# Layer 0's projections: from F32R pairs to two scaled F16 parts, with the weights and W_out's rows in a ring of seven places

## Chip, core and metric

The kernel runs on one core of a Trainium2 chip. The metric is the device time of one execution in microseconds (us); lower is better. The engines are named as the profile names them: PE (matrix multiply), PEld (its weight loads), DVE (VectorE), ACT (ScalarE), POOL (GpSimd), and SP, whose queue issues nearly all transfers. Each engine works off its own list of instructions strictly in order.

## What is computed

Two decoder layers on a 1024x1024 input `x` (1024 tokens, width 1024). The change is in layer 0, forgetting attention (FoX) with 16 heads of 64:

```python
h = rmsnorm(x, norm_g[0])
q, k, v, f, z = split(h @ w_in)              # w_in: 1024 x (4*1024 + 16)
c = cumsum(log_sigmoid(f + b_f))             # the forget gate, per head
logits = q @ k.T * 64**-0.5 + c[query] - c[key], causal
x = x + ((softmax(logits) @ v) * silu(z)) @ w_out
```

Layer 1 (native sparse attention) and the final norm follow; the diff changes there only how the square sums of its weights are taken beforehand.

## The kernel before

Every large product is made from two parts of each operand, `hi` and `lo` (`lo` is what `hi` lost in rounding), as three matmuls: hi·hi, hi·lo, lo·hi (`mm3`, L269 to L271 of the profile). In layer 1 both parts are F16, and the weights are first multiplied by a power of two worked out from the root of their square sums, so that they fit F16's range. In layer 0 the parts are F32R, four bytes each, and need no scale.

*Opening.* Eight tiles of 128 tokens are normed (`Norm`, L97 to L109), transposed on PE (L119) and split by `to_hT` into `hT`, the transposed activations (L123 on ACT, L124 on DVE). The order on PE, DVE and ACT is written out by hand here (`manual_schedule`). From tile 5 on, the projection `k0` and the gate (`forget_gate`, matmuls `pf<-hT,wf`) are mixed in.

*Sections.* There are eight head pairs `p`, and four weight sections for each, in the order k, v, q, z: 32 sections of 1024x128. A section is loaded (512 KB), split into `whi` (DVE, L131) and `wlo` (POOL, L134, four pieces), and used in two halves of 512 tokens by `project`: 8 x 3 matmuls of 128x512 for each half, so 48 for a section and 1536 in all. One place `wst` holds the section just loaded; `whi` and `wlo` have two places each.

*Attention.* `fox_main` runs 64 `FoxDuo`s: scores `S` (L767, L768, still F32R), exp (ACT L785), parts `hl` (ACT L786, DVE L787), a transposing transfer (SP L788), and two duos later the product with `v` (`O`, L801 and L802). `merge` puts the projections of later head pairs (`fox_fill`) between the duos by a ratio of costs written in the code; these costs are not changed. The tile framework's scheduler then orders each engine; `late_on` (`keep_in_program_order`) pins an instruction at its place.

*Gate.* After `pf`'s last matmul the gate's values go through a transfer (`fg<-fT`), a chain of small operations on DVE with an Exp and a Ln on ACT (L436 to L454), one tiny matmul `pc<-fg,below` (L457), and DVE L458 and L459. The result `cD` is the bias `B` of the scores.

*Squares.* `early` (class `Squares`) loads W_out and most of layer 1's weights once ahead, 256 KB at a time, for their square sums: ACT L183, which the scheduler places after a small ACT operation (`zg`, L182) on the section's newest result.

*W_out's rows* for layer 0's output product are loaded and converted by `load_wout16` (L703; ACT L712, DVE L714, POOL) into the places of `hT` when the last projections have left them, and `out_start0` begins the product.

Of the kernel before, what the change touches and what calls it, by code (L numbers as in the profile page):

```python
# [41 lines left out]
def tile_fox_nsa(ctx, tc, a, out):  # L42
# [72 lines left out]
    def to_hT(h, t, hT, name, ps=(ps_t, ps_t)):  # L115
        for c in range(2):
            pt = ps[c](f"pth_{name}_{c}")
            for j in range(4):
                T.transpose(pt[:, j * P:(j + 1) * P], h[:, (4 * c + j) * P:(4 * c + j + 1) * P], ident)  # L119
            hi = hT[t // 4][0][:, 4 * c:4 * c + 4, t % 4 * P:(t % 4 + 1) * P]  # L120
            lo = hT[t // 4][1][:, 4 * c:4 * c + 4, t % 4 * P:(t % 4 + 1) * P]
            v = pt.rearrange("p (k t) -> p k t", k=4)
            A.copy(hi, v)  # L123
            V.tensor_tensor(lo, v, f(hi) if hi.dtype == F32R else hi, OP.subtract)  # L124

    def load_w(pool, src, name):
        st = pool.tile([P, KC, P], F32, tag="wst", bufs=1, name=f"wst_{name}")
        dma(st, src)
        hi = pool.tile([P, KC, P], F32R, tag="whi", bufs=2, name=f"whi_{name}")
        lo = pool.tile([P, KC, P], F32R, tag="wlo", bufs=2, name=f"wlo_{name}")  # L130
        V.tensor_copy(hi, st)  # L131
        for k in range(0, KC, 2):
            c = slice(k, k + 2)
            G.tensor_tensor(lo[:, c], st[:, c], f(hi[:, c]), OP.subtract)  # L134
        return hi, lo
# [23 lines left out]
    sums = consts.tile([P, 65], F32, name="sums")  # L159

    class Squares:


        def __init__(self, pool, items, size, bufs):
# [3 lines left out]
        def load(self):  # L168
            if self.items:
                src, col = self.items.pop(0)  # L170
                k, c = src.shape[1:]
                t = self.pool.tile([P, self.size], F32, tag="sq", bufs=self.bufs, name=f"sq_{col}")[:, 0:k * c]
                dma(t.rearrange("p (k c) -> p k c", k=k), src)
                self.at.append((t, col))

        def step(self, x):
            if self.bufs > 1:
                self.load()
            if self.at:
# [3 lines left out]
                A.activation(t, t, AF.Square, bias=z, accum_out=(self.out if col < 8 and self.bufs > 1 else sums)[:, col:col + 1])  # L183
            if self.bufs == 1:
                self.load()
# [18 lines left out]
    def gain_scale(gB):  # L204
# [3 lines left out]
        u = consts.tile([P, 4], F32, name="gain")  # L208
# [4 lines left out]
        V.tensor_scalar(r.bitcast(I32), m.bitcast(I32), 0x7F800000, None, OP.bitwise_xor)  # L213
        V.tensor_scalar(gB, gB, r, 2.0 ** 8, OP.mult, OP.mult)
        V.tensor_scalar(e, m, 2.0 ** -9, None, OP.mult)
# [9 lines left out]

    late_on = tc.keep_in_program_order
# [78 lines left out]
    def channel_scale(sc, n, undo):  # L305
# [8 lines left out]
        V.tensor_scalar(e, e, 2.0 ** -15 * undo, None, OP.mult)  # L314
# [100 lines left out]
    bf = st.tile([H, 1], F32, name="bf")  # L415
    below = st.tile([P, P], F32, name="below")
    wf = st.tile([P, KC, P], F32R, name="wf")
    G.tensor_copy(wf, zero[:, :, None].to_broadcast([P, KC, P]))

    def forget_gate():  # L420
        fT = st.tile([H, S], F32, name="fT")
        f2 = st.tile([H, S], F32, name="f2")
        for half in range(2):
# [6 lines left out]
            V.tensor_copy(f2[:, ts], pt[32:32 + H, :])  # L430
            V.scalar_tensor_tensor(fT[:, ts], pt[0:H, :], bf, f2[:, ts], OP.add, OP.add)
# [33 lines left out]
    def fox_k(p):  # L465
# [3 lines left out]
        for half in range(2):  # L469
# [12 lines left out]
            if p:  # L482
                early.step(pt[:, 0:1])
# [3 lines left out]
    def opening():  # L487
        gB = st.tile([P, D], F32, name="gB")
        xs = []
        for t in range(NT):  # L490
# [4 lines left out]
            if t == 1:  # L495
                wst = wp.tile([P, KC, P], F32, tag="wst", bufs=1, name="wst_k0")
                dma(wst, a["fox_w"][8])
            if t == 3:
                dma(wfst, a["fox_w_f"].rearrange("(k p) c -> p k c", p=P))
                dma(bf, a["fox_b_f"].rearrange("o h -> h o"))  # L500
                dma(below, a["below"])
        dma(tri, a["tri"])
        whi = wp.tile([P, KC, P], F32R, tag="whi", bufs=2, name="whi_k0")
        wlo = wp.tile([P, KC, P], F32R, tag="wlo", bufs=2, name="wlo_k0")
        side = []
        hs = {}
        with tc.manual_schedule(engines={T.engine, V.engine, A.engine}):
            for t in range(NT + 1):
                if t < NT:
                    nm = Norm(st, xs[t], f"n0_{t}", 3)  # L510
                    nm.square(slice(0, D))
                    hs[t] = nm.finish(gB)
                if t:
                    to_hT(hs.pop(t - 1), t - 1, hT, f"n0_{t - 1}", (ps_s, ps_t))
                if t == 1:
                    V.tensor_copy(whi, wst)
                    G.tensor_tensor(wlo, wst, f(whi), OP.subtract)
# [24 lines left out]
    def fox_v(p):  # L542
# [5 lines left out]
        for half in range(2):  # L548
# [27 lines left out]

    def fox_z(p, w, halves=(1, 0)):
# [6 lines left out]
        for half in halves:  # L584
# [1320 lines left out]
```

## Time and profile before

| | |
|---|---|
| median of 3 runs | 1456.75 us (1456.5 to 1458.18) |
| the profiled execution | 1458.12 us; its span, first to last instruction, 1456.2 us |
| PE busy | 1368.0 us, 94% of the span |
| DVE, ACT, POOL busy | 1120.3 (77%), 915.9 (63%), 585.3 us (40%) |
| HBM read | 120.31 MB |

How to read it: a group's row gives its busy time, the mean duration of one, and the idle time of its engine just ahead of it with the instruction that ended it. Matmuls overlap: a matmul's duration is longer than the time until the next one starts, so the pace of PE is read from the starts in the timeline. A row of stages gives the length of the stretch, the busy time of PE, PEld, DVE, ACT and POOL with their instruction counts, the clock that PE was granted, the share of time in which the transfer engines were busy, and GB/s.

### The profile page before, as it was taken

What the parts mean: (1) busy time and instruction counts of PE and PEld (TensorE: products, weight loads), DVE (VectorE), ACT (ScalarE), POOL (GpSimd) and SP (SyncE); (2) the same over time, 40 slices, a digit from 0 to 9 for tenths busy, and PEclk for the clock granted to TensorE, in tenths of its full rate; (3) what the DMA queues carried; (4) which work ended last, traced back from release to release, by engine and by line L of the source; (5) the groups of instructions that cost most, each with busy time, mean ns of one, the idle gap of its engine ahead of it and who ended that gap; (6) DMA issues with size and microseconds to landing.
All of it is one profiled execution on the core that took longest, in us unless ns stands there. A gap on an engine that the chain in (4) does not pass through costs nothing. (4 is left out here: it accounts for less than half of the span.)

```text
span 1456.2 us, 30393 instructions
## 1 busy us (share of the span) xinstructions
PE 1368.0 (94%) x10499; PEld 928.0 (64%) x10499; DVE 1120.3 (77%) x3016; ACT 915.9 (63%) x2328; POOL 585.3 (40%) x781
## 2 busy tenths in 40 slices
PE   5999999999999989999999988889999999998998
PEld 4778888888888745445545544446666766666643
DVE  6587787787878698486757677878999899989834
ACT  5376667776767665155555475667877778778512
POOL 2142433434334251231203456245766766765500
PEclk9999999999999999999999999999999999999999
DMA  5379798898988999354654446454667676776434
GB/s 197 96 164 191 188 185 199 203 186 198 189 197 180 244 230 203 107 176 151 189 174 141 134 121 159 119 148 92 135 151 164 140 171 123 135 169 150 95 109 145
DMA packets 414922, 234.72 MB, mean 161 GB/s; under 512 B 334448, under 2 KB 372656, under 8 KB 414768
## 3 DMA queue, kind: packets, MB, share of 16 engines
q1 hardware_dynamic: 414768, 232.78, 67.1%
q8 instruction: 83, 1.36, 0.4%
q14 instruction: 71, 0.58, 0.1%
HBM read 120.31 MB, written 28.38 MB: 102 GB/s over the span
## 5 line engine op out<-in xcount | busy, mean ns | idle before, releaser
L1662 PE MATMUL S_n<-nk,nq 128*128 128x320 f16 (+5 forms) x768 | 154.6, 314 | 13.5 <-DVE m_n L1670 12.6
L785 ACT ACTIVATE P<-P,m 128x512 f32<-128x512 f32 (+1 forms) x192 | 116.3, 607 | 53.9 <-DVE m L776 52.6
L1677 POOL TENSOR_TENSOR hl_n<-P_n,hl_n 128x640 f16<-128x640 f32 (+4 forms) x128 | 144.8, 1132 | 10.0
L756 POOL TENSOR_TENSOR Bd<-B,tri 128x128 f32<-128x128 f32 x128 | 62.4, 502 | 205.8 <-DVE m L776 189.3
L787 DVE SCALAR_TENSOR_TENSOR hl<-P,hl 128x512 f16<-128x512 f32 (+1 forms) x192 | 116.0, 620 | 28.7 <-ACT hl L786 27.2
L1676 POOL CAST hl_n<-P_n 128x640 f16<-128x640 f32 (+4 forms) x128 | 76.4, 597 | 122.1 <-ACT P_n L1673 97.3
L1673 ACT ACTIVATE P_n<-P_n,m_n 128x640 f32<-128x640 f32 (+7 forms) x128 | 98.7, 771 | 30.2 <-DVE m_n L1670 29.6
L1673 ACT ACTIVATE P_n<-P_n,m_n,units 128x640 f32<-128x640 f32 (+4 forms) x128 | 100.1, 782 | 22.5 <-DVE m_n L1672 20.6
L1662 PEld LDWEIGHTS <-nq 128*128 128x128 f16 x768 | 71.4, 98 | 60.4 <-issue 25.5
L286 ACT ACTIVATE pth_n<-ptp_n 128x512 f16<-128x512 f32 (+1 forms) x160 | 85.1, 545 | 38.9 <-PE ptp_n L1695 38.3
L287 DVE SCALAR_TENSOR_TENSOR ptl_n<-ptp_n,pth_n 128x512 f16<-128x512 f32 (+1 forms) x160 | 99.6, 632 | 7.9 <-ACT pth_n L286 5.9
L1695 PE MATMUL ptp_n<-ident,P_n 128*128 128x128 f32 x576 | 93.2, 279 | 7.5 <-ACT P_n L1673 2.2
L786 ACT ACTIVATE hl<-P 128x512 f16<-128x512 f32 (+1 forms) x192 | 92.4, 512 | 1.9 <-DMA pT<-hl 0.5
L1670 DVE CUSTOM_DVE_ANT_0 P_n<-S_n,wmask 128x640 f32<-128x640 f32 (+4 forms) x128 | 83.1, 650 | 7.2 <-PE S_n L1662 6.3
L1695 PEld LDWEIGHTS ptp_n<-ident,P_n 128*128 128x128 f32 x576 | 64.9, 141 | 33.4 <-DVE ptl_n L287 7.3
L183 ACT ACTIVATE sq<-sq,zg 128x512 f32<-128x512 f32 (+2 forms) x73 | 59.5, 815 | 22.8 <-DMA sq<-in_nsa_w_dram 17.8
L1703 PE MATMUL O_n<-nv,pth_n 128*128 128x64 f16 x576 | 71.7, 193 | 1.0 <-ACT pth_n L286 0.6
L97 ACT ACTIVATE h_n<-xr 128x512 f32<-128x512 f32 x32 | 20.0, 625 | 83.6 <-DVE xr L1795 41.4
L1704 PE MATMUL O_n<-nv,pth_n 128*128 128x64 f16 x576 | 71.8, 193 | 0.0
L1670 DVE CUSTOM_DVE_ANT_0 P_n<-S_n,bias,units 128x640 f32<-128x640 f32 (+1 forms) x64 | 68.8, 1074 | 2.9 <-PE S_n L1662 2.3
L1705 PE MATMUL O_n<-nv,ptl_n 128*128 128x64 f16 x576 | 68.7, 193 | 0.9 <-DVE ptl_n L287 0.9
L767 PE MATMUL S<-KH,Q 128*128 128x512 f32 (+1 forms) x192 | 65.0, 354 | 2.6 <-DVE m L776 2.3
(514 smaller groups left out, 4731.6 us busy)
## 6 DMA issues: line engine op xcount, KB each, us to landing
sq<-in_nsa_w_dram SPq DMA_DIRECT2D x40, 256.0 KB
B<-cD SPq DMA_DIRECT2D x16, 512.0 KB
nq<-qD SPq DMA_DIRECT2D x64, 128.0 KB
x<-in_x_dram SPq DMA_DIRECT2D x8, 512.0 KB
wst_k<-in_fox_w_dram SPq DMA_DIRECT2D x8, 512.0 KB
wst_v<-in_fox_w_dram SPq DMA_DIRECT2D x8, 512.0 KB
sq<-in_fox_w_out_dram SPq DMA_DIRECT2D x16, 256.0 KB
wst_q<-in_fox_w_dram SPq DMA_DIRECT2D x8, 512.0 KB
```

The lines of the kernel that those rows point to most:

```text
L286: A.activation(hi[:, 0:n], pt[:, 0:n], AF.Copy, scale=scale)
L287: V.scalar_tensor_tensor(lo[:, 0:n], pt[:, 0:n], scale, h, OP.mult, OP.subtract)
L785: A.activation(L[:, 0:n], L[:, 0:n], AF.Exp, bias=init, scale=-1.0, accum_out=self.lr[:, col + c:col + c + 1])
L786: A.activation(hi[:, cs], L[:, 0:n], AF.Copy, scale=UP)
L787: V.scalar_tensor_tensor(lo[:, cs], L[:, 0:n], UP, hi[:, cs], OP.mult, OP.subtract)
L1662: T.matmul(ps[:, b, 0:w], self.q[x][:, qi * P:(qi + 1) * P], k[:, k0 + b * w:k0 + b * w + w], start=(x == 0), stop=(x == 1))
L1670: V.tensor_tensor_reduce(dst, src, mk, 1.0 if y else unit, 3e38, OP.add, OP.min, m)
L1673: A.activation(L, L, AF.Exp, bias=m, scale=minus if y else -1.0, accum_out=self.l[:, y, qi:qi + 1])
L1676: G.tensor_copy(hl[:, 0:n], L)
L1677: G.tensor_tensor(hl[:, n:2 * n], L, hl[:, 0:n], OP.subtract)
L1695: T.transpose(pt[:, (x + i) * P:(x + i + 1) * P], L[:, kb * P - k0:(kb + 1) * P - k0], ident)
L1704: T.matmul(o, hi, v[:, 64:128], start=False, stop=False)
```

## The change

- `hT` becomes F16, and `to_hT` multiplies by a scale from the largest gain: `gain_scale(gB, 0)`, one reduction and five small DVE operations, now in the opening.
- Each weight section is scaled as it is split, by `split_w16`: DVE makes `hi` with a multiply; POOL multiplies the section in place and then subtracts (four pieces each). `k0`'s section is split on DVE alone.
- The scale of a head pair's four sections comes from their square sums: `ring_square` (ACT, 128x1024, one for each section), `ring_total` (ACT cast, a PE matmul with `ones`), `ring_scale` (five small DVE operations). The inverse is applied where q, k, v and z are read out of PSUM, in operations that were there before; k's and q's together in q's.
- Sections and, after them, the eight 512 KB pieces of W_out's rows go through `ring`, seven places of 4 KB per partition; `issue()` loads the next item. `conv_wout` converts W_out's rows straight from the ring.
- `early` loads 512 KB at a time, pinned squares without the `zg` operation, half as many.

```diff
-    hT = [[hp.tile([P, KC, 512], F32R, ...) for i in range(2)] for x in range(2)]
+    hT = [hp.tile([P, 2, KC, 512], F16, tag=f"h{x}", name=f"hT0_{x}") for x in range(2)]
...
+    def issue():
+        if len(ring) < len(items):
+            src, name = items[len(ring)]
+            ring.append(hp.tile([P, KC, P], F32, tag=f"r{len(ring) % 7}", name=f"wst_{name}"))
+            dma(ring[-1], src)
...
+    def ring_square(n):
+        j = sa.tile([P, D], BF16, tag="sq", bufs=1, name=f"wj_{n}")
+        late_on(A.activation(j, ring[n]..., AF.Square, accum_out=wu[n // 4][:, n % 4:n % 4 + 1]))
+    def ring_total(p, x, y):
+        A.copy(tb[:, x:y], wu[p][:, x:y])
+        late_on(T.matmul(pt[:, x:y], ones, tb[:, x:y], start=True, stop=True))
+    def split_sec(n):
+        return split_w16(ring[n], wu[n // 4][:, 5 + n % 4:6 + n % 4], parts, n > 0)
...
+    def tick(second):
+        n = sect[0]
+        if second:
+            if n % 4 == 2 and n < 28:
+                ring_scale(n // 4 + 1, 0, 4, totals.pop())
+            early.load()
+            sect[0] += 1
+        else:
+            if n + 6 < 32:
+                ring_square(n + 6)
+            early.square()
+            if n % 4 == 2 and n < 28:
+                totals.append(ring_total(n // 4 + 1, 0, 4))
...
             if p == 0:
-                for _ in range(11):
+                issue()
+                early.load()
+                for n in (1, 2, 3):
+                    ring_square(n)
+                    for _ in range(3):
+                        yield next(gate0)
+                pt = ring_total(0, 1, 4)
+                for _ in range(2):
                     yield next(gate0)
+                ring_scale(0, 1, 4, pt)
...
-                rows0 = load_wout16(hp, "fox_w_out", 1, 200, 2)
-                yield next(rows0)
+                rows0 = conv_wout(1, 200, 2)
```

The place that moves most is the start of head pair 0's v. On PE, before: the last of the gate's matmuls, then v's; `pc` stands behind all 48 of v's matmuls.

```order
L427 MATMUL pf_395<-hT_1_0_103,wf 128x512
L428 MATMUL pf_395<-hT_1_1_104,wf 128x512
L269 MATMUL v_0_457<-hT_0_0_101,whi_v_439 128x512
L270 MATMUL v_0_457<-hT_0_1_102,whi_v_439 128x512
L271 MATMUL v_0_457<-hT_0_0_101,wlo_v_440 128x512
...
L457 MATMUL pc<-fg_418,below 128x1
L269 MATMUL q_1_545<-hT_1_0_103,whi_q_448 128x512
```

PE at the same place now (F16 weights are loaded by an instruction of their own; `wsum` is `ring_total`'s matmul):

```order
L493 MATMUL pf_442<-hT_1_102,wf 128x512
L427 LDWEIGHTS ones
L427 MATMUL wsum_1_465<-wtb_1_463,ones 128x3
L522 MATMUL pc<-fg_473,below 128x1
L267 LDWEIGHTS whi_v_503
L267 MATMUL v_0_529<-hT_0_101,whi_v_503 128x512
L268 LDWEIGHTS whi_v_503
L268 MATMUL v_0_529<-hT_0_101,whi_v_503 128x512
L269 LDWEIGHTS wlo_v_504
L269 MATMUL v_0_529<-hT_0_101,wlo_v_504 128x512
```

`wsum` and `pc` moved ahead of v's 48 matmuls.

DVE there before: the gate's chain ends (L454), and the split of z follows; v's and q's had been made long before.

```order
L453 SCALAR_TENSOR_TENSOR fg_418<-fg_417,fg_416 128x4
L454 TENSOR_TENSOR fg_415<-fg_415,fg_418 128x96
L131 CAST whi_z_538<-wst_z_536 128x1024
L458 COPY fg_416<-pc 128x1
L459 TENSOR_SCALAR fg_415<-fg_415,fg_416 128x128
```

DVE now (`wu` holds the sums and scales of the sections):

```order
L518 SCALAR_TENSOR_TENSOR fg_473<-fg_472,fg_471 128x4
L519 TENSOR_TENSOR fg_470<-fg_470,fg_473 128x96
L436 TENSOR_SCALAR wu_103<-wsum_1_465 128x3
L523 COPY fg_471<-pc 128x1
L437 TENSOR_SCALAR wu_103<-wu_103 128x3
L439 TENSOR_SCALAR wu_103<-wu_103,gain_162 128x3
L438 TENSOR_SCALAR wu_103<-wu_103 128x3
L524 TENSOR_SCALAR fg_470<-fg_470,fg_471 128x128
L441 SCALAR_TENSOR_TENSOR wu_103<-wu_103 128x2
L140 TENSOR_SCALAR whi_v_503<-wst_v_140,wu_103 128x1024
```

The scales of v, q and z, and with them v's `hi`, stand behind the gate's whole chain.

In the opening, DVE between tile 3's norm and tile 4's before (`st_n` and `h_n` are a tile's norm; `k0`'s one cast stands further ahead, its `lo` was POOL's):

```order
L109 SCALAR_TENSOR_TENSOR h_n_3_187<-x_120,st_n_3_186,gB 128x1024
L124 TENSOR_TENSOR hT_0_1_102<-pth_n_2_0_192,hT_0_0_101 128x4x128
L124 TENSOR_TENSOR hT_0_1_102<-pth_n_2_1_199,hT_0_0_101 128x4x128
L105 RECIPROCAL st_n_4_206<-st_n_4_206 128x1
L109 SCALAR_TENSOR_TENSOR h_n_4_207<-x_125,st_n_4_206,gB 128x1024
```

The same stretch now (`fu` holds the scales of `k0` and of the gate's weights):

```order
L128 SCALAR_TENSOR_TENSOR hT_0_101<-pth_n_2_1_228,gain_162,hT_0_101 128x4x128
L593 TENSOR_SCALAR fu<-wsum_235 128x2
L595 TENSOR_SCALAR fu<-fu 128x2
L596 TENSOR_SCALAR fu<-fu 128x2
L597 TENSOR_SCALAR wu_103<-fu,gain_162 128x1
L598 TENSOR_SCALAR wu_103<-fu,gain_162 128x1
L140 TENSOR_SCALAR whi_k_242<-wst_k_122,fu 128x1024
L149 SCALAR_TENSOR_TENSOR wlo_k_243<-wst_k_122,fu,whi_k_242 128x512 x2
L105 RECIPROCAL st_n_4_247<-st_n_4_247 128x1
L109 SCALAR_TENSOR_TENSOR h_n_4_248<-x_131,st_n_4_247,gB 128x1024
```

Eight operations on `k0`'s weights and scales now stand ahead of tile 4's norm. In the rest of layer 0 the order of projections, scores and products on PE stays as it was but for a handful of matmuls that change places with a neighbour.

More of the change, by code (lines that the diff above doesn't have):

```diff
@@ L122, in to_hT @@
             v = pt.rearrange("p (k t) -> p k t", k=4)
[L123 to L135, printed above, removed]
+            if scale is None:
+                A.copy(hi, v)
+                V.tensor_tensor(lo, v, hi, OP.subtract)
+            else:
+                A.activation(hi, v, AF.Copy, scale=scale)
+                V.scalar_tensor_tensor(lo, v, scale, hi, OP.mult, OP.subtract)
     def load_w16(staged, src, name, scale, gp=False):
@@ L202, in roots, with gain_scale @@
         return r
-    def gain_scale(gB):
-        u = consts.tile([P, 4], F32, name="gain")
+    def gain_scale(gB, layer):
+        u = (consts if layer else hp).tile([P, 4], F32, name=f"gain{layer}")
         m, r, e, b = (u[:, i:i + 1] for i in range(4))
@@ L482, in fox_k @@
             if p:
-                early.step(pt[:, 0:1])
+                tick(half)
         ready["k", p] = KH, KL
@@ L646, in fox_fill @@
                 assert not early.at
-                first.append(roots(sums[:, 0:41], ((0, 4), (4, 8), (8, 24), (24, 40), (40, 41)), "early"))
-                ready["o7"] = hp.tile([P, NT, 2, P], F16, tag="h11", name="o7_0")
-                yield from out_start0(load_wout16(hp, "fox_w_out", 0, 200, 0))
+                first.append(roots(sums[:, 0:21], ((0, 2), (2, 4), (4, 12), (12, 20), (20, 21)), "early"))
+                issue()
+                ready["o7"] = hp.tile([P, NT, 2, P], F16, tag="r0", name="o7_0")
+                yield from out_start0(conv_wout(0, 200, 0))
     xs0 = {}
     def out_start0(rows1):
-        yield next(rows1)
         parts = [(t, 0, 4) for t in (4, 5, 6, 7)] + [(t, 4, 7) for t in (4, 5, 6, 7)] + [(t, 0, 7) for t in (0, 1, 2)]
@@ L695, in out_start0, with conv_rows, conv_wout @@
                 yield 1000
+    def conv_rows(src, w, half, pace, vrows):
+        for k in range(4):
+            r = 4 * (1 - half) + k
+            sc = ready["wscale"][:, r:r + 1]
+            for c in range(2):
+                yield pace
+                cs = slice(c * 512, c * 512 + 512)
+                A.activation(w[:, 0, k, cs], src[k][:, cs], AF.Copy, scale=sc)
+                if c or k < vrows:
+                    V.scalar_tensor_tensor(w[:, 1, k, cs], src[k][:, cs], sc, w[:, 0, k, cs], OP.mult, OP.subtract)
+                else:
+                    G.tensor_scalar(src[k][:, cs], src[k][:, cs], sc, 1.0, OP.mult, OP.mult)
+                    G.tensor_tensor(w[:, 1, k, cs], src[k][:, cs], w[:, 0, k, cs], OP.subtract)
+        ready.setdefault("wout", []).append((w[:, 0], w[:, 1]))
+    def conv_wout(half, pace, vrows):
+        src = [ring[36 - 4 * half + k].rearrange("p k c -> p (k c)") for k in range(4)]
+        w = hp.tile([P, 2, 4, D], F16, tag=f"h{half}", name=f"wo0_{half}")
+        yield from conv_rows(src, w, half, pace, vrows)
     def load_wout16(pool, src, half, pace, vrows):
```

167 lines of the change are left out of this document (102 added, 65 removed).

## The prediction

> **What bounds the kernel now.** I read the stages first, then who waited for whom on PE in layer 0, then the timeline for PE's pace, and last the gate's chain, because the order shows that PE will wait for it. The stages (columns: window, length, busy PE, PEld, DVE, ACT, POOL, then the clock, the transfer engines' share, GB/s):
>
> ```profile
> span 1456.2 us, 30393 instructions
> 110.00:500.00 390.00, 389.67 (x2427) 316.38 (x2426) 299.18 (x947) 270.07 (x720) 142.83 (x218) 1.00 0.87 193
> 500.00:590.00 90.00, 77.88 (x517) 46.23 (x516) 73.43 (x231) 51.22 (x130) 25.36 (x34) 0.94 1.01 232
> 1000.00:1300.00 300.00, 287.80 (x3690) 204.11 (x3690) 273.60 (x748) 232.61 (x547) 197.68 (x237) 1.00 0.68 143
> ```
>
> From 110 to 500 us PE is busy without a gap, DVE 77%, ACT 69%, POOL 37%. In those 390 us PE waited once (columns: engine and line, for whom, total, times, longest):
>
> ```profile
> PE z L271 <- POOL wlo_z L134: 0.2, 1, 0.2
> ```
>
> So there PE's own pace sets the time, and what makes its matmuls start closer together is gained in full until another engine is late. Its pace is read from starts (start, duration), F32R first, F16 below:
>
> ```profile
> 45.11 0.40 PE L427 MATMUL pf<-hT,wf 128*128 128x512 f32 x1
> 48.61 0.40 PE L428 MATMUL pf<-hT,wf 128*128 128x512 f32 x1
> 48.84 0.39 PE L269 MATMUL v<-hT,whi_v 128*128 128x512 f32 x1
> 714.14 0.38 PE L270 MATMUL pn_qr<-hT,whi_nqr 128*128 128x512 f16 x1
> 720.83 0.38 PE L271 MATMUL pn_qr<-hT,wlo_nqr 128*128 128x512 f16 x1
> ```
>
> Between the first and second row lie 15 intervals: 3.50/15 = 0.2333 us. Between the two F16 rows lie 31: 6.69/31 = 0.2158. An F16 matmul of this shape thus costs PE 0.0175 us less.
>
> The Trainium skill, "TensorE: Matmul & The Clock Gate", section "Back-to-back issue gap", gives N/2.4 + 2.5 ns for a warm array and no term for the data type; that is 216 ns for 512 columns. F16 agrees with it; F32R, by 0.2333 us, does not. By the rule the change would gain nothing in pace; by the rows it does, and the rows decide.
>
> **Part 1: up to q0's start, +14.2.** The time lost is in the start of head pair 0. The gate's chain before:
>
> ```profile
> 49.76 0.74 DVE L431 SCALAR_TENSOR_TENSOR fT<-pf,bf,f 16x512 f32<-16x512 f32 x1
> 53.24 0.29 DVE L436 SCALAR_TENSOR_TENSOR fg<-fg 128x128 f32<-128x128 f32 x1 [2.74 <-DMA fg<-fT]
> 55.97 1.28 ACT L443 ACT_TABLE_LOAD   x1
> 57.61 0.29 DVE L444 TENSOR_TENSOR fg<-fg,fg 128x128 f32<-128x128 f32 x1 [1.88 <-ACT fg L443]
> 59.40 0.26 DVE L454 TENSOR_TENSOR fg<-fg,fg 128x96 f32<-128x96 f32 x1
> 60.04 0.28 PE L457 MATMUL pc<-fg,below 128*128 128x1 f32 x2
> 60.18 0.48 PE L269 MATMUL q<-hT,whi_q 128*128 128x512 f32 x1
> 60.86 0.85 DVE L459 TENSOR_SCALAR fg<-fg,fg 128x128 f32<-128x128 f32 x1
> 605.34 0.15 DVE L211 TENSOR_SCALAR gain<-gain 128x1 f32<-128x1 f32 x1
> ```
>
> Before, v's 48 matmuls (48.84 to 60.04) covered this chain, and nobody on PE saw it. Now `pc` and v's split stand behind it, so the cover is gone: PE finishes `pf`, and then waits for all of it.
>
> (a) The opening. DVE gets the gain's reduction and five small operations, five more for `k0`'s scale, and two subtractions that POOL did. What it loses is a stall: POOL's long subtraction ran at 13.28, and DVE's norm of a tile beside it took 3.40 us where the next one took 1.28.
>
> ```profile
> 13.28 2.34 POOL L517 TENSOR_TENSOR wlo_k<-wst_k,whi_k 128x1024 fp32r<-128x1024 f32 x1 [10.70 <-DVE st_n L105]
> 13.31 3.40 DVE L109 SCALAR_TENSOR_TENSOR h_n<-x,st_n,gB 128x1024 f32<-128x1024 f32 x1
> 18.01 1.28 DVE L109 SCALAR_TENSOR_TENSOR h_n<-x,st_n,gB 128x1024 f32<-128x1024 f32 x1
> 604.10 1.21 DVE L210 TENSOR_REDUCE gain<-gB 128x1 f32<-128x1024 f32 x1
> 9.92 0.17 DVE L105 RECIPROCAL st_n<-st_n 128x1 f32<-128x1 f32 x1 [1.44 <-ACT st_n L104]
> L183 ACT ACTIVATE sq<-sq,zg 128x1024 f32<-128x1024 f32 x16 | 18.4, 1148 | 0.4
> L183 ACT ACTIVATION_READ_ACCUMULATOR sq<-sq,zg 128x1 f32 x73 | 13.6, 187 | 0.0
> L787 DVE SCALAR_TENSOR_TENSOR hl<-P,hl 128x512 f16<-128x512 f32 (+1 forms) x192 | 116.0, 620 | 28.7 <-ACT hl L786 27.2
> ```
>
> Added on DVE: 1.21 + 10 x 0.15 + 2 x 0.62 = 3.95; gone: 3.40 - 1.28 = 2.12; so +1.8. Of it the idle 1.44 ahead of tile 1's reciprocal may hide most (+0.4). On ACT one 1024-wide square with its read (1.15 + 0.19) and a few small operations (the gate's square, two casts, about 0.8 at a quarter of a us each) stand ahead of tile 3's norm: up to +2.1 more, so +0.4 to +3.9. I take +3.0, near the upper end, since DVE and ACT both have little air there. Some 70 F16 matmuls until `pf`'s end give back 70 x 0.0175 = 1.2. `pf` ends at 48.84 + 1.8 = 50.6.
>
> (b) The wait. From `pf`'s end to the end of L454: 59.66 - 48.84 = 10.8. The Ln's table load stood behind v's readout on ACT, which now comes later, so DVE's idle 1.88 goes: 8.9. Then the scales: six small operations, with issue about 0.19 each (1.1), L524 (the L459 of before: between 0.29, the chain's other 128x128 operations, and its own 0.85 beside POOL's work; 0.4, as POOL is idle now), and v's `hi`, 0.75:
>
> ```profile
> L147 DVE TENSOR_SCALAR whi_nqr<-wst_nqr,roots_early x6: 752/755/1192, 706.5 to 793.1; 128x1024 f16<-128x1024 f32 x6
> L151 POOL TENSOR_SCALAR wst_nv<-wst_nv,roots_late x16: 476/482/906, 809.4 to 852.2; 128x256 f32<-128x256 f32 x16
> L152 POOL TENSOR_TENSOR wlo_nv<-wst_nv,whi_nv x16: 666/674/1116, 810.3 to 853.3; 128x256 f16<-128x256 f32 x16
> L134 POOL TENSOR_TENSOR wlo_z<-wst_z,whi_z x32: 731/741/1200, 60.9 to 481.1; 128x256 fp32r<-128x256 f32 x32
> ```
>
> Together 11.2; at least 10.2, with the scales wholly beside other work, at most 13.5, if the 1.88 stays and L524 takes 0.85. v's first matmul: 50.6 + 11.2 = 61.8.
>
> (c) v itself. Its third matmul needs POOL's first `lo` piece, 0.48 + 0.48 + 0.67 = 1.6 after `hi`, and after eleven idle us PE starts at half clock, as `k0` did:
>
> ```profile
> 23.92 0.78 PE L269 MATMUL k<-hT,whi_k 128*128 128x512 f32 x1
> 28.27 0.40 PE L270 MATMUL k<-hT,whi_k 128*128 128x512 f32 x1
> ```
>
> Ten intervals there took 4.35 instead of 2.33: +2.0. The two overlap; I take +2.2 for both (2.0 to 3.6). All of v then: 48 x 0.2158 + 2.2 = 12.6, q0's start at 74.4 against 60.18: **+14.2**, with the bounds above +10.4 to +18.
>
> **Part 2: PE's pace from there on, -29.7.** Left are 1536 - 48 (k0) - 48 (v0) = 1440 projection matmuls: 1440 x 0.0175 = **-25.2**. Besides, a weight load of F32R is long, and the first projection after a product pays for it:
>
> ```profile
> 301.92 0.19 PE L802 MATMUL O<-v,pT 128*128 128x64 f16 x1
> 301.95 0.49 PE L269 MATMUL q<-hT,whi_q 128*128 128x512 f32 x1
> 302.27 0.40 PE L270 MATMUL q<-hT,whi_q 128*128 128x512 f32 x1
> L269 PEld LDWEIGHTS q<-hT,whi_q 128*128 128x128 f32 x128 | 24.4, 190 | 5.4
> L269 PEld LDWEIGHTS <-whi_nqr 128*128 128x128 f16 x96 | 9.6, 100 | 10.6 <-issue 1.1
> ```
>
> 0.32 instead of 0.233 us; the F16 load is shorter by as much, 0.09. The order has 52 such passages: **-4.5** (between nothing and that; the load's difference accounts for all of it). The scores stay F32R.
>
> **Part 3: the other engines in that stretch, +4.** ACT: in these 390 us 50 squares of 512 with their reads and `zg` cost 50 x (0.724 + 0.187 + 0.2) = 56; now some 25 early and 28 ring squares of 1024, 53 x 1.34 = 71, and a few casts: 270 + 17 = 287 of 360.
>
> ```profile
> L183 ACT ACTIVATE sq<-sq,zg 128x512 f32<-128x512 f32 x50 | 36.2, 724 | 18.6 <-DMA sq<-in_nsa_w_dram 15.9 <-DMA sq<-in_fox_w_out_dram 1.4
> ACT sq L183 <- DMA sq<-in_nsa_w_dram: 17.8, 9, 6.3
> ```
>
> DVE: 299 + 7 x 5 x 0.15 = 304 of 360, 85%. POOL: for each section 4 x (0.48 + 0.67 - 0.74) = 1.6 more, 26 sections: +43, 186 of 360; it came late for PE once in 390 us, by 0.2 (above), so this alone delays nobody. `ring_total`'s cast stands on ACT a section ahead of its matmul, and that matmul costs PE a narrow slot seven times. The transfers stay the same in bytes; half as many square loads go through SP. In layer 1 DVE at 91% (273.60 of 300) goes with 4% of idle PE, while at 77% in layer 0 there is none. Between, at 85% of 360, I take 1%: **+4** (0 to 14).
>
> **Part 4: the end of layer 0, -1.5.** From 500 to 590 PE idles 90 - 77.88 = 12 us. W_out's 4 MB now come earlier, and two squares fewer stand in ACT's way; the conversions are as many. -5 to +1.
>
> **Sum:** 14.2 - 25.2 - 4.5 + 4 - 1.5 = -13.0 on the profiled execution's 1458.12: 1445.1. That execution lies 1.4 above the median of the runs, 1456.75; on that scale 1443.7, said as **1444**.
>
> **Rivals.** *R1, the full gain:* no engine is late (+0), the opening hides its work and the start costs +11: 1456.75 + 11 - 29.7 - 3 = 1435. For it: PE's single wait in 390 us. Against: the order, which leaves nothing beside the chain.
>
> *R2, DVE becomes the second bound:* POOL's extra 43 us block DVE as at 13.31 us. If every us did, DVE would have 304 + 43 = 347 of 360, above layer 1's 91%, where 4% of PE was idle: +14 instead of +4, so 1454. For it: the 3.40. Against: that was one 1024-wide operation beside DVE's own; POOL's pieces are 0.5 to 0.7 long. The skill's "SBUF — State Buffer", section "Who interferes with whom", says that such operations hold a shared port to their end; the 3.40 agrees, and no run here counts how often.
>
> *R3, slower: the squares' loads come late.* 512 KB are now asked for half a section (390/26/2 = 7.5 us) before a pinned square, where 256 KB were; ACT waits in order, and the exps behind it. Before, nine squares waited 17.8 us, the longest 6.3. ACT's 287 leave 73 of 360; slower than before it would get when the 25 early squares wait over (73 + 13)/25 = 3.5 us each. At 4.5: ACT's stretch is 287 + 112 = 399, so nothing of part 2 is left: 1456.75 + 14.2 + 9 - 1.5 = 1478; at 3.7 about 1460.
>
> *R4, no change in pace in layer 0:* F32R's 0.2333 comes from something that F16 shares there: 1456.75 + 14.2 - 4.5 + 4 - 1.5 = 1469. This is what the clock-gate page's rule would give. Against: the same interval at 45 us and 300 us, in streams of different content.
>
> **How the numbers follow.** The forecast, PE's pace less the gate's wait, 1437 to 1451: 60%. R1 14%, R2 14%, R3 7%, R4 2%, others 3%. Changes of up to 0.2% (2.9 us) are about what a measurement cannot tell from none: faster means below 1453.8. Forecast and R1 are faster; R2 straddles the line (6 faster, 5 same, 3 slower); so 81% faster, 6% same, 13% slower. The range, 1431 to 1456, takes in R1, the forecast's bounds and most of R2 and leaves out R3 and R4.
>
> **What would show it.** PE idle for about 11 us near 51 to 62 us, released by DVE's `hi` of v or by `pc`; intervals of 0.216 in q, k, v, z; PE still without gaps of note from 120 to 470; ACT's waits for the squares' transfers below 1 us each. Wrong would be: PE waiting for DVE or ACT all through the stretch, intervals of 0.233, or v starting near 50.

## The result, and the profile after

The changed kernel takes 1469.95 us, median of five runs (1466.27 to 1473.78), where the kernel before took 1456.75 (1455.81 to 1459.36) beside it: ratio 1.0085, interval 1.0062 to 1.0108. It is slower by 0.85%; the forecast was 0.9% faster. The profiled execution took 1467.63 us, 9.5 more than the one before.

The page after (span and busy times), and the two stages of layer 0 (columns as before):

```profile
span 1465.8 us, 30457 instructions
PE 1342.5 (92%) x10508; PEld 786.3 (54%) x10508; DVE 1130.9 (77%) x3069; ACT 933.7 (64%) x2291; POOL 648.7 (44%) x904
110.00:500.00 390.00, 370.53 (x2444) 205.87 (x2443) 312.26 (x996) 278.51 (x678) 204.75 (x331) 1.00 0.90 195
500.00:590.00 90.00, 82.94 (x574) 47.33 (x573) 80.26 (x254) 55.30 (x138) 26.47 (x36) 0.98 0.88 191
```

PE is busy 25.5 us less in sum and the kernel is longer all the same. From 110 to 500 us PE did 370.53 of 390 where it had done 389.67: it got its faster matmuls, and stood still for 19.5 us where it had stood still for 0.3.

One ruler serves for all that follows. It is the view of one tile, `wlo_q` on PE; each row has min, median and longest duration (ns), then the start of the first and of the last such matmul. The first lies at q0's start, the last near the end of the projections. Before, then after:

```profile
L271 PE MATMUL q<-hT,wlo_q x128: 389/392/632, 60.7 to 514.2; 128*128 128x512 f32 x128
L269 PE MATMUL q<-hT,wlo_q x128: 377/379/379, 73.9 to 523.9; 128*128 128x512 f16 x128
```

The first starts 13.2 later. The stretch from first to last is 450.0 where it was 453.5: 3.5 shorter, where PE's pace alone (part 2) was worth 29.7. The last starts 9.7 later, and so does the end, by 9.5. So the loss is the start's, which was forecast, plus some 26 us in the stretch, of which 4 were forecast. The row of the whole stretch, before and after (columns as before):

```profile
60.70:514.20 453.50, 449.74 (x2773) 364.51 (x2772) 344.88 (x1103) 312.80 (x833) 164.49 (x254) 1.00 0.87 194
73.90:523.90 450.00, 425.18 (x2780) 235.09 (x2779) 353.20 (x1133) 318.61 (x776) 226.65 (x366) 1.00 0.87 190
```

PE's busy time fell by 24.6 us, and its idle time rose from 3.8 to 24.8: 21 of the 26 are waits.

The start, from PE's timeline after (start, duration, in brackets the idle time and who ended it):

```profile
48.62 0.38 PE L493 MATMUL pf<-hT,wf 128*128 128x512 f16 x1
51.51 0.16 PE L427 MATMUL wsum<-wtb,ones 128*128 128x3 bf16 x1 [2.52 <-ACT wtb L425]
57.56 0.56 PE L522 MATMUL pc<-fg,below 128*128 128x1 f32 x2 [5.88 <-issue]
59.57 0.61 PE L267 MATMUL v<-hT,whi_v 128*128 128x512 f16 x1 [1.45 <-DVE whi_v L140]
61.66 0.61 PE L269 MATMUL v<-hT,wlo_v 128*128 128x512 f16 x1 [1.06 <-POOL wlo_v L145]
73.51 0.38 PE L267 MATMUL q<-hT,whi_q 128*128 128x512 f16 x1
```

PE waits for the sums, for the gate's chain (put down to "issue": what it needs came just before), for `hi`, and for POOL's first `lo`, and begins v at half clock (0.61 us for a matmul of 0.38).

What PE waited for from 110 to 500 us, after; before, there was one wait of 0.2 us in all:

```profile
PE O L903 <- DMA pT<-hl: 9.7, 7, 3.1
PE O L903 <- DVE m L878: 3.6, 2, 2.6
PE S L869 <- DVE m L878: 2.5, 6, 0.9
```

The largest part is the product `O` waiting for its transposing transfer `pT`. These transfers stand in SP's queue, and so do the loads of sections. SP's own waits in the same window, first before, then after (rows for POOL's `lo` of k, v and z only):

```profile
SPq L128 <- POOL wlo_k L134: 14.1, 6, 3.2
SPq L128 <- POOL wlo_v L134: 11.0, 6, 2.9
SPq L128 <- POOL wlo_z L134: 8.8, 5, 2.3
```

```profile
SPq L413 <- POOL wlo_k L145: 21.0, 6, 4.5
SPq L413 <- POOL wlo_z L145: 19.0, 7, 5.8
SPq L413 <- POOL wlo_v L145: 10.7, 5, 3.1
```

33.9 us have become 50.7. A load takes the place of the section that POOL is just splitting, and may be issued only when POOL's last `lo` piece is done. POOL's work on a section is longer now (POOL was busy for 204.75 us of the window where it had been for 142.83), so the load, and each transposing transfer behind it in the queue, goes out later. One such case in the timeline, after:

```profile
277.26 1.34 DVE L889 SCALAR_TENSOR_TENSOR hl<-P,hl 128x512 f16<-128x512 f32 x2
278.84 1.30 POOL L145 TENSOR_TENSOR wlo_k<-wst_k,whi_k 128x256 f16<-128x256 f32 x2
280.16 0.33 SPq L413 DMA_DIRECT2D wst_z<-in_fox_w_dram  x1
280.58 3.44 SPq L890 DMA_TRANSPOSE pT<-hl  x1
286.11 0.23 PE L903 MATMUL O<-v,pT 128*128 128x128 f16 x1 [1.20 <-DMA pT<-hl]
```

`hl` is ready at 278.60; POOL's pieces end at 280.14; SP issues the load, and the transposing transfer only at 280.58, two us after its data. At 286.11 the product waits 1.20 us. A duo has two such issues; over duos 10 to 50 of the 64 they came 0.55 us after their data on average before, and 1.47 after.

### The profile page after: what moved, and what is told of

Read it like the earlier page. It is cut to its first block, busy times and chain, and to the rows that moved or that the text cites. A ratio compares the mean times of both kernels' runs of the same rounds, so it can differ in the third digit from the quotient of the medians.

```text
span 1465.8 us, 30457 instructions
## 1 busy us (share of the span) xinstructions
PE 1342.5 (92%) x10508; PEld 786.3 (54%) x10508; DVE 1130.9 (77%) x3069; ACT 933.7 (64%) x2291; POOL 648.7 (44%) x904
## 5 line engine op out<-in xcount | busy, mean ns | idle before, releaser
L858 POOL TENSOR_TENSOR Bd<-B,tri 128x128 f32<-128x128 f32 x128 | 66.1, 531 | 161.2 <-DVE m L878 116.2
L869 PE MATMUL S<-KH,Q 128*128 128x512 f32 (+1 forms) x192 | 76.7, 414 | 5.7 <-DVE m L878 2.5
L903 PE MATMUL O<-v,pT 128*128 128x128 f16 x576 | 58.5, 221 | 19.6 <-DMA pT<-hl 16.0
## 6 DMA issues: line engine op xcount, KB each, us to landing
sq<-in_nsa_w_dram SPq DMA_DIRECT2D x28, 512.0 KB
B<-cD SPq DMA_DIRECT2D x16, 512.0 KB
x<-in_x_dram SPq DMA_DIRECT2D x8, 512.0 KB
wst_k<-in_fox_w_dram SPq DMA_DIRECT2D x8, 512.0 KB
wst_v<-in_fox_w_dram SPq DMA_DIRECT2D x8, 512.0 KB
wst_q<-in_fox_w_dram SPq DMA_DIRECT2D x8, 512.0 KB
wst_z<-in_fox_w_dram SPq DMA_DIRECT2D x8, 512.0 KB
```

## The experiments

The table has every run: its time, its ratio to the kernel before beside it, and the ruler. (Ratios compare best between rows; the kernel before itself ran at 1456.75 to 1458.67 us beside them. The ruler is read from one profiled execution of each kernel, so differences of two or three us between its rows say little.)

| kernel | us | ratio (interval) | q0 | last | stretch |
|---|---|---|---|---|---|
| before | 1456.75 | 1 | 60.7 | 514.2 | 453.5 |
| after | 1469.95 | 1.0085 (1.0062 to 1.0108) | 73.9 | 523.9 | 450.0 |
| f16only | 1440.80 | 0.9868 (0.9846 to 0.9889) | 58.1 | 499.4 | 441.3 |
| noscale | 1456.52 | 0.9986 (0.9967 to 1.0006) | 75.2 | 514.2 | 439.0 |
| early0 | 1460.98 | 1.0017 (0.9998 to 1.0036) | 65.2 | 518.1 | 452.9 |
| spread | 1463.22 | 1.0033 (1.0017 to 1.0049) | 75.0 | 522.0 | 447.0 |
| even | 1477.33 | 1.0129 (1.0102 to 1.0156) | 73.9 | 536.4 | 462.5 |
| evenf16 | 1455.83 | 0.9977 (0.9963 to 0.9991) | 57.7 | 518.1 | 460.4 |
| poolmul | 1461.81 | 1.0018 (1.0003 to 1.0034) | 57.9 | 515.7 | 457.8 |
| poolwst2 | 1457.48 | 0.9995 (0.9982 to 1.0008) | 57.8 | 514.5 | 456.7 |
| f16wst2 | 1437.99 | 0.9869 (0.9847 to 0.9892) | 58.4 | 494.0 | 435.6 |
| later | 1468.31 | 1.0071 (1.0045 to 1.0097) | 75.5 | 528.5 | 453.0 |
| comb | 1453.04 | 0.9963 (0.9950 to 0.9976) | 63.6 | 508.8 | 445.2 |
| nomul | 1456.25 | 0.9977 (0.9959 to 0.9995) | 73.7 | 512.5 | 438.8 |
| gpq | 1468.38 | 1.0060 (1.0036 to 1.0084) | 75.7 | 523.5 | 447.8 |
| poolgpq | 1458.56 | 1.0007 (0.9985 to 1.0028) | 58.6 | 512.0 | 453.4 |
| f16gpq | 1447.43 | 0.9914 (0.9886 to 0.9941) | 58.7 | 503.4 | 444.7 |
| combnomul | 1435.28 | 0.9846 (0.9811 to 0.9880) | 61.4 | 493.0 | 431.6 |
| f16sq64 | 1434.97 | 0.9830 (0.9800 to 0.9860) | 58.0 | 493.3 | 435.3 |

PE's pace alone would make the stretch 453.5 - 29.7 = 423.8.

**F16 alone (f16only).** The kernel before, with F16 for `hT`, `whi`, `wlo` and `wf`, no scales and no ring; each engine's instructions keep their order.

```diff
-hT = [[hp.tile([P, KC, 512], F32R, ...
+hT = [[hp.tile([P, 2, KC, 512], F16, ...)[:, 0] ...
-hi = pool.tile([P, KC, P], F32R, tag="whi", ...)
+hi = pool.tile([P, 2, KC, P], F16, tag="whi", ...)[:, 0]
```

> The kernel before with one thing changed: hT, whi, wlo and the gate's weights are F16 instead of F32R, without any scales, squares, ring or moved work (its small parts lose accuracy, its instructions are those of before). Theory A, the vector engines' pace: in a run of duos DVE and ACT need about 6.9 us for a duo, as much as PE needed with F32R, so a faster PE only waits: PE idles 10 to 20 us between 110 and 500 us, where it idled 0.3, and the time is 1437 to 1447. Theory B, the added work is to blame: without it PE follows at its F16 pace, idles under 5 us there, and the time is 1425 to 1433.

16 us faster, and 2.6 of it before q0 (on the ruler). Its stretch is 12.2 shorter, not 29.7: more than half of the pace was lost with none of the change's added work there. Its window from 110 to 500 us, its last 19.4 us of the stretch, what PE waits for in the window, and what ACT waits for most:

```profile
110.00:500.00 390.00, 374.43 (x2463) 208.53 (x2462) 300.24 (x971) 275.82 (x740) 136.06 (x220) 0.99 0.92 203
480.00:499.40 19.40, 13.09 (x81) 6.39 (x80) 12.15 (x47) 11.51 (x32) 1.77 (x4) 0.82 1.06 290
PE total_o L243 <- ACT sb_o L241: 5.9, 1, 5.9
PE S L767 <- DVE m L776: 2.4, 6, 1.0
PE O L801 <- DMA pT<-hl: 2.2, 3, 1.5
ACT sq L183 <- DMA sq<-in_nsa_w_dram: 24.1, 9, 6.4
```

15.6 us idle: PE now arrives before DVE, ACT and what they feed. The largest wait is a single one: at 493.47 PE stands 5.9 us for a total that layer 0's output product needs, and around it the granted clock fell too (0.82 in the last 19.4 us). The rest is short waits. The averages (DVE 77%, ACT 71%) hide a lag that may be behind them, since the work of those engines comes in runs. The eight duos of a run follow each other every 6.9 us before, and at F16's pace every 6.4 where PE doesn't wait; then, about 16 us after the last duo's start, the next run begins. Within a run DVE and ACT fall behind: the time from a duo's last score to its last `hl`, averaged over the five runs of duos 10 to 49, grows from 5.1 us at a run's first duo to 7.4 at most before (6.6 over all); in f16only from 5.7 to 8.4 (7.6 over all), and after from 6.0 to 9.0 (8.1 over all, the longest 10.5). The window of one run before shows no more than this:

```profile
226.00:270.00 44.00, 44.00 (x285) 35.83 (x284) 34.14 (x113) 33.34 (x90) 11.47 (x20) 1.00 0.90 200
```

DVE at 78%, ACT at 76%: neither is full even there. They take turns in a duo (maximum, exp, `hl`), so each waits for the other, and a chain can fall behind before an engine is full. A rival stands beside this: ACT, in order, waits in f16only for the transfers of the early squares, with the exps behind them, for 25.5 us of the 390 (the 24.1 above and 1.4 for W_out's; 17.3 before). No run here takes that away from f16only.

**Three things taken out of the changed kernel.** *noscale:* head pairs 1 to 7 use head pair 0's scales, so the ring's squares, sums and scales go.

```diff
-ring_scale(n // 4 + 1, 0, 4, totals.pop())
-ring_square(n + 6)
-totals.append(ring_total(n // 4 + 1, 0, 4))
-return split_w16(ring[n], wu[n // 4][...
+return split_w16(ring[n], wu[0][...
```

> The changed kernel without the squares, sums and scales of the sections from head pair 1 on (they use head pair 0's scales): 28 squares of 1024 on ACT, 28 reads, 7 casts, 7 matmuls and 35 small DVE operations are gone. Theory A: the loop of DVE and ACT over a duo is little shorter, PE's idle between 110 and 500 us falls from 19.5 to 12 to 18, the time to 1462 to 1468. Theory B: it falls under 6, the time to 1453 to 1457.

13 us gained; on the ruler 11 of it in the stretch (439.0 from 450.0).

*early0:* head pair 0's squares stand ahead of `k0`'s end, and its scales ahead of most of the gate's chain.

```diff
+for n in (1, 2, 3): ring_square(n)
 yield from k0
-for n in (1, 2, 3): ring_square(n) and three steps of the gate each
+three steps of the gate
 pt = ring_total(0, 1, 4)
-two steps of the gate
 ring_scale(0, 1, 4, pt)
+eight steps of the gate
```

> The changed kernel with head pair 0's three squares ahead of k0's end and its sum and scales ahead of the gate's chain, so that v's split no longer stands behind it. If the wait at the start costs what the trace shows (v's first matmul 59.6 instead of 48.8, and some 2 us at half clock), q0 starts at 60 to 63 instead of 73.5 and the time falls by 9 to 13, to 1457 to 1461. The rival, that the time is given back at the first scores, because the gate's result or the vector engines are late then: 1463 to 1469.

9 us gained, most of the price of the order at the start: q0 comes 8.7 us earlier on the ruler, at 65.2, still 4.5 later than before. In its timeline v begins right behind the gate's matmuls again (the last of them starts at 49.76); what is left are a wait of 1.14 us for POOL's first `lo` at 51.71, and `pc`'s:

```profile
47.36 0.17 PE L427 MATMUL wsum<-wtb,ones 128*128 128x3 bf16 x1
49.98 0.38 PE L267 MATMUL v<-hT,whi_v 128*128 128x512 f16 x1
64.08 0.40 PE L522 MATMUL pc<-fg,below 128*128 128x1 f32 x2 [2.27 <-DVE fg L518]
```

*spread:* the early square moves from the half in which the ring's square stands to the other half.

```diff
 early.load()  # second half's tick
+  ahead of it: early.square()
 ring_square(n + 6)  # first half's tick
-early.square()
```

> The changed kernel with its two 1024-wide squares of a section in different halves of it, instead of one behind the other. If a block of 2.5 us on ACT ahead of the exps makes PE wait, PE's idle between 110 and 500 us falls from 19.5 to under 12 and the time by 6 to 10, to 1460 to 1464. If ACT's and DVE's sum over a run of duos counts, it is within 3 us of the changed kernel, 1467 to 1472.

6.7 us gained. In the changed kernel the two squares stood together on ACT, ahead of the exps:

```profile
96.40 1.04 ACT L421 ACTIVATE wj<-wst_v 128x1024 bf16<-128x1024 f32 x1
97.44 1.04 ACT L174 ACTIVATE sq<-sq 128x1024 f32<-128x1024 f32 x1
98.48 0.50 ACT L887 ACTIVATE P<-P,m 128x256 f32<-128x256 f32 x1
100.39 0.29 PE L903 MATMUL O<-v,pT 128*128 128x128 f16 x1 [3.69 <-DMA pT<-hl]
```

The exp of the next duo starts two us late, and a product finds its transfer missing in the same stretch.

**More even spacing (even, evenf16).** Other numbers in the ratio of costs, on the changed kernel and on f16only: a wider spacing of the duos and a shorter stretch of lone projections at a pair's end.

```diff
-PACE = 2.3
+PACE = 2.5
-yield 1000   -> yield 500
-yield 450    -> yield 225
```

> The changed kernel with another mix of the same work: PACE 2.5 instead of 2.3 and the two pairs of costs 1000 and 450 at a head pair's end halved, so that 21 to 24 projection matmuls stand ahead of a duo's scores (21 before) and 39 instead of 57 at the head pair's end. Theory A: duos come every 6.4 to 6.9 us instead of 6.4, and DVE and ACT keep up better: PE's idle between 110 and 500 us falls from 19.5 to 8 to 14, the time to 1458 to 1465. The rival, that the waits come from single late steps (squares ahead of exps), wherever the duos stand: 1467 to 1472. Or the shorter stretch at the pair's end makes PE wait for the product's transposes (pto), as long or longer.

> The kernel before in plain F16 (the run with nothing but the data type changed) with the same other mix. Theory A: of its 15.6 us of idle PE between 110 and 500 us about half goes; 1432 to 1437 after 1440.8. If its waits don't hang on the spacing of the duos: 1439 to 1443.

Both are slower, by some 7 and 15 us: if runs are the trouble, this was not the way to break them. The first scores of a pair now came too soon behind its `Q`. PE's waits from 110 to 500 us have a new top row, in even and in evenf16:

```profile
PE S L869 <- DVE Q L655: 6.6, 2, 3.7
```

```profile
PE S L767 <- DVE Q L573: 8.5, 3, 4.4
```

The stretch at a pair's end is needed to bring up the next pair's q and k. Yet waits are not the whole price. The stretch of even:

```profile
73.90:536.40 462.50, 438.06 (x2804) 240.76 (x2803) 362.66 (x1157) 323.49 (x785) 227.79 (x368) 0.97 0.88 188
```

PE idles 24.4 us in it, no more than in the changed kernel (24.8), but its mean granted clock was 0.97 instead of 1.00; 3% of 462.5 us is some 14 us, by this estimate as much as the stretch grew (12.5). In evenf16 PE idles 25.7 us (16.4 in f16only) at a clock of 0.97 (0.99). The theory of runs is neither shown nor refuted by these two.

**POOL's multiply, added to F16 alone (poolmul).** 124 multiplies by one, each a piece in place, ahead of POOL's subtractions; DVE and ACT keep their order.

```diff
+G.tensor_scalar(st[:, c], st[:, c], 1.0, 1.0, OP.mult, OP.mult)
 G.tensor_tensor(lo[:, c], st[:, c], hi[:, c], OP.subtract)
```

> The kernel before in plain F16, and one thing more: POOL multiplies every piece of a section (by one) ahead of its subtraction, as the changed kernel does. That is 124 more POOL operations of about 0.5 us. If POOL's work blocks DVE (the second rival of the prediction), DVE's operations get longer and the time goes up by 5 to 15 us, to 1446 to 1456. If it runs beside the others, it is within 2 us of plain F16, 1439 to 1443.

21 us slower than f16only, back past the kernel before. Its stretch is 457.8 (441.3 without), longer than with F32R. SP's waits for POOL, and the rows of f16only to compare (second fence):

```profile
SPq L128 <- POOL wlo_k L135: 18.6, 6, 4.2
SPq L128 <- POOL wlo_v L135: 17.5, 6, 4.4
SPq L128 <- POOL wlo_z L135: 12.5, 5, 4.8
```

```profile
SPq L128 <- POOL wlo_k L134: 9.1, 6, 2.5
SPq L128 <- POOL wlo_v L134: 7.6, 5, 2.1
SPq L128 <- POOL wlo_z L134: 6.4, 4, 2.1
```

23.1 us have become 48.6, about as in the changed kernel (50.7). POOL was 47% busy in the window, and for PE itself its `lo` was late by 1.0 us in all. The transposing transfers' issue, 0.61 us after its data in f16only, is at 0.92.

**Attempts to give SP air.** *poolwst2* and *f16wst2* give the section loaded a second place in poolmul and f16only; *later* loads each section one section later in the changed kernel.

```diff
-st = pool.tile([P, KC, P], F32, tag="wst", bufs=1, ...)
+st = places[nplace[0] % 2]     # two halves of one free tile
```

```diff
 if p == 0:
-    issue()
     early.load()
...
-issue()
+issue(); issue()   # at the last section
```

> Plain F16 with POOL's extra multiply, and two places for the loaded section instead of one. Theory C, SP's queue: the load of the next section waits on SP until POOL's last piece has left the only place, and the transposing transfers of the exps queue behind it; POOL's multiply lengthens that by 2 us and more a section. With a second place SP waits no more for POOL (in 110 to 500 us it waited some 55 us for it), and most of the 21 us that the multiply cost come back: 1440 to 1448 after 1461.8. The rival, that POOL's multiply costs by its own time (DVE blocked, or bias and lo pieces late): 1456 to 1463.

> Plain F16 with two places for the loaded section instead of one, the multiply left out. Theory C: SP waited some 28 us for POOL between 110 and 500 us there too; the time falls from 1440.8 to 1432 to 1438. If the waits of PE that were left come from the pace of DVE and ACT alone: 1439 to 1442.

> The changed kernel with each load of the ring issued one section later, six ahead instead of seven, so that it goes to a place that POOL has left long ago. Theory C: SP's waits for POOL (55 us between 110 and 500) go, PE's idle there falls from 19.5 to 8 to 14, the time by 6 to 13, to 1457 to 1464. If DVE's and ACT's pace sets the waits: 1467 to 1472.

As tests of the queue, all three are void. The two places lie in one tile, and SP's waits for POOL stayed (62 us from 76 to 500 in poolwst2, 29 in f16wst2); with one load fewer ahead, the place a load asks for in later is still that of the section just split (61 us). So their -4, -3 and -2 us say nothing on the queue. f16wst2 has the ratio of f16only; that its time lies in theory C's range is no support.

**The multiply out, or the loads on another queue.** *nomul:* the changed kernel without POOL's multiply; `lo` is then not the section's rest. *gpq, poolgpq, f16gpq:* the loads of sections go on POOL's own queue, in the changed kernel, in poolmul and in f16only.

```diff
-G.tensor_scalar(st[:, c], st[:, c], scale, ...)     # nomul
...
-dma(ring[-1], src)
+G.dma_start(ring[-1], src)   # gpq, from the eighth load on; poolgpq, f16gpq: all but the first
```

> The changed kernel without POOL's multiply of the sections (its small parts are then wrong numbers). If the multiply costs in the changed kernel what it cost in plain F16 (20 us): 1448 to 1455. If there other waits take its place: 1460 to 1468.

> The changed kernel with the ring's loads (from the eighth on) issued by POOL's queue instead of SP's, so that SP never waits for POOL's pieces. Theory C: the transposing transfers go out when their data are ready; PE's idle between 110 and 500 us falls from 19.5 to 8 to 13, the time to 1455 to 1463. If POOL's own time counts: 1467 to 1473.

> Plain F16 with POOL's extra multiply and the sections' loads on POOL's queue. Theory C: most of the 21 us of the multiply come back, 1440 to 1449. If POOL's own time counts: 1456 to 1463.

> Plain F16 with the sections' loads on POOL's queue. Theory C: SP's 28 us of waits for POOL go, 1434 to 1439 after 1440.8. Without an effect of SP: 1439 to 1443.

nomul gains 13.7 us; SP's waits for POOL's k, v and z fall to 28.9. With the loads on POOL's queue the transposing transfers go out sooner (0.39 us after their data on average in gpq, 1.47 in the changed kernel), yet gpq gains only 1.6, inside the noise, and all three runs miss theory C's times. The move itself costs f16only 6.6 (f16gpq; the two intervals just touch). Two places where it may cost are seen: in gpq the 26 issues in the window keep POOL itself busy for 15.7 us, and SP's store of `o`, in the queue of the transposing transfers, now waits for POOL for 25.0 us, 10.0 in the changed kernel.

```profile
SPq L936 <- POOL o L934: 25.0, 9, 6.4
```

With the loads on POOL's queue the multiply costs 1458.56 - 1447.43 = 11 us, on SP's 21 (by the ratios 14 and 22, each with some 4 or 5 either way). So by this a third to a half of its price went through SP's queue, and the rest is POOL's work itself; that the move costs the same with and without the multiply is assumed, and no run shows it. Lateness of the issue is not a price by itself either: in comb, below, it is 1.58 us.

A part of that rest is seen. A DVE operation that reads two operands from SBUF is longer beside POOL: in the changed kernel's duos 10 to 50, `hl` of 128x512 took 0.686 us alone (34 times) and 0.829 on average beside a POOL operation (27 times), while `P<-S` of the same size, which reads one of its operands from PSUM, did not change (0.749 alone and 0.747 beside). An example in the timeline:

```profile
254.32 0.93 POOL L144 TENSOR_SCALAR wst_z<-wst_z,wu 128x256 f32<-128x256 f32 x2
254.86 0.94 DVE L889 SCALAR_TENSOR_TENSOR hl<-P,hl 128x512 f16<-128x512 f32 x1
284.47 0.69 DVE L889 SCALAR_TENSOR_TENSOR hl<-P,hl 128x512 f16<-128x512 f32 x1 [0.20 <-ACT hl L888]
```

The Trainium skill, "SBUF — State Buffer", section "Who interferes with whom", says that a DVE instruction with two SBUF inputs contends with a GpSimd instruction that reads SBUF, and one with a single SBUF input, outside the two-port modes, does not; these numbers agree. In sum it is little: over duos 10 to 50 the multiply lengthens DVE's operations by 3.4 to 5.3 us (four pairs of kernels). How the rest of the 11 us comes about is open.

**All together.** *comb* is early0, spread and later at once in the changed kernel. *combnomul* takes POOL's multiply out of it as well (as in nomul). *f16sq64* is f16only with the early squares over 64 of their 512 columns, so ACT's part of them shrinks.

```diff
+if self.bufs == 1: t = t[:, 0:64]                       # f16sq64, ahead of the early square
```

> The changed kernel with three edits together: head pair 0's scales ahead of the gate's chain (9 us by itself), the two squares of a section in different halves (6.7 us), and the ring's loads one section later. If they add up: 1443 to 1450, faster than the kernel before; if they take the same waits away, 1452 to 1458.

> The run with the three edits together (1453.0), and POOL's multiply left out as well (wrong small parts). If the costs add up, 13 us less: 1437 to 1443, the time of plain F16. If they are the same waits counted twice: 1445 to 1452.

> Plain F16 with the early squares taken over 64 columns instead of 512 (the loads stay; the scales of layer 1's weights and of W_out come out of an eighth of the squares): about 0.46 us less on ACT for each of 50 squares between 110 and 500 us, 23 in all. If the pace of ACT and DVE makes PE wait: its idle there falls from 15.6 to 5 to 9 and the time from 1440.8 to 1431 to 1437. If single late steps do: 1439 to 1443.

comb, which computes all that the changed kernel does, takes 1453.04 us, ratio 0.9963: it beats both kernels. Without the multiply it falls by another 17.8 to 1435.28, the figure of the rival R1, so the start (9.0 alone), the two squares (6.7), `later` (1.6) and the multiply (13.7) add up, to 34.7 where they sum to 31.0. combnomul's stretch is 431.6, shorter than f16only's 441.3, though DVE and ACT do more in the window there. f16sq64 gains 5.8 on f16only (their intervals overlap a little), with ACT at 262.66 instead of 275.82 of the 390 us. combnomul, then f16sq64:

```profile
110.00:500.00 390.00, 380.89 (x2547) 214.77 (x2546) 319.83 (x1040) 290.99 (x703) 142.09 (x226) 1.00 0.93 203
110.00:500.00 390.00, 376.18 (x2495) 210.84 (x2494) 306.22 (x993) 262.66 (x752) 136.20 (x222) 1.00 0.93 206
```

An engine at 71% was on the path: taking 13 us of ACT's work off gave about 6 us of time back (some operations of ACT and DVE also change places in f16sq64). But PE's idle time in the window fell only from 15.6 to 13.8, where 5 to 9 were expected, and the single wait for the output product's total is still 5.0 of it. And combnomul, with DVE at 82%, ACT at 75% and the lag rising from 5.1 to 8.5 within a run, leaves PE idle for only 9.1 us: mean share and lag alone don't say how much PE waits. What sets it apart from f16only is, among other things, that ACT's waits for the squares' transfers are 1.2 us there, not 25.5.

## Why the prediction was wrong, by its own steps

| step | forecast | measured (profiled executions) |
|---|---|---|
| 1, up to q0 | +14.2 | +13.2 |
| 2 and 3, the stretch | -29.7 + 4 | -3.5 |
| 4, from there to the end | -1.5 | -0.2 |
| sum | -13.0 | +9.5 |

*Part 1, right.* `pf` ended at 48.84, not 50.6, as the opening hid its work; the wait to v was 10.7 (forecast 11.2); v took 13.9 (12.6), since POOL and the half clock cost a little more. The misses of 1.8 and 1.3 us cancel in part, so the closeness of the sum is partly luck. The naming of the gate's chain as the lost cover holds, and early0 shows that the order set most of the price.

*Part 2, right as to pace.* F16 intervals are 0.216 us in q, k, v and z (73.51, 73.72, 73.94), and the first projection behind a product costs 0.217 instead of 0.32. PE's busy time in the stretch fell by 24.6 us, and by 28.4 in combnomul (421.32 from 449.74), near the 29.7. The mechanism of R4 is refuted. The formula of the Trainium skill, "TensorE: Matmul & The Clock Gate", section "Back-to-back issue gap", that the prediction cites gives 216 ns; F16 in layer 0 agrees with it, as it did in layer 1.

*Part 3 failed.* Its +4 (0 to 14) measured about 26. Taking out the multiply and parting the squares (combnomul) brings the stretch to 431.6, so 18 of the 26 hang on these two (early0 and `later`, which are in combnomul as well, did not shorten it by themselves: 452.9 and 453.0). Three sentences of it fell:

- "at 85% of 360, I take 1%": the share of DVE was set against layer 1's. A share over 390 us is a mean over runs of duos and lone projections; f16only lost 17 of the 29.7 with DVE at 77%. Why is open: shown is that PE waits for what DVE and ACT feed; that the two set the limit in turn is argued from the lag, and that less work on ACT gives 5.8 back rests on intervals that overlap a little. The waits of ACT for the squares' transfers, and the one of 5.9 us, are rivals.
- POOL "it came late for PE once in 390 us, by 0.2 (above), so this alone delays nobody": I looked only at who on PE waits for POOL. SP waits for POOL too, and had done so for 38.6 us before, in plain sight of its waits. Behind SP's load stand the transposing transfers, for which PE waits. The multiply costs 14 to 21 us (nomul, poolmul), by the queue only in part. POOL's added work was undersized too: forecast +43 us in the window, measured +62 (204.75 from 142.83).
- ACT was summed ("287 of 360") and not looked at for where the squares stand: two in a row ahead of the exps cost 6.7 (spread), and all of the scales' work 13 (noscale), which overlap with the rest.

*Part 4* was small either way: -0.2 for a forecast of -1.5; why is not shown.

*The rivals.* R4's 1469 lies nearest to the measured 1469.95, but by luck: it had no gain in pace and little loss, where the runs show the gain and a larger loss. R2 (1454) had POOL in it, but its mechanism, POOL stopping DVE, is 3 to 5 us, and the queue was not in it. R3 named a time on this side too (1460 to 1478), and its mechanism is refuted for the changed kernel: ACT's waits for the squares' transfers fell from 17.3 us to 1.8, one wait.

```profile
ACT sq L174 <- DMA sq<-in_nsa_w_dram: 1.8, 1, 1.8
```

R1's figure, 1435, is what comb without the multiply reaches, by other means than R1 said.

## What to carry to other kernels

Before you promise PE's pace in full, look for each stage at more than the feeding engines' mean share: how far they lag behind PE at the end of a burst, and what they themselves wait for. Either may keep the pace from being had in full. Give longer work to a helper engine only after asking every queue that waits for it, the transfer queue above all, and what stands behind the wait there. Keep single long operations on a feeding engine apart, and put a chain of scales where other matmuls cover it.

## What the runs showed of the hardware that was not expected

A queue that issues transfers in order turns a wait for one load into lateness of the transfers behind it: 0.55 us against 1.47 on average here. Moving the loads to POOL's queue was not free: 6.6 us in f16gpq. And a wait of PE of 3.69 us (at 100.39, above) cost more than its length: the projections behind it began at half clock, as the timeline after shows,

```profile
101.82 0.61 PE L267 MATMUL z<-hT,whi_z 128*128 128x512 f16 x1
103.31 0.38 PE L268 MATMUL z<-hT,whi_z 128*128 128x512 f16 x1
```

while behind the wait of 1.20 us at 286.11 they kept their 0.38, and so they did behind one of 3.11 us that ended at 117.9. In even, by the estimate above, such spells made up most of the loss.
